# First FFN of a two-layer backbone on one core: modulation sums by accumulating DMAs, paced accumulations, and a joint K sweep

## The chip, the cores and the metric

The kernel runs on one core of one Trainium2 chip. The metric is the device time of one execution in microseconds (us). The kernel before took 1245.69 us, the median of three runs (1245.28 to 1246.67). The profile comes from a further execution of the same program; its own time stands in the table below.

## The reference, cut to what matters

Two streams of 256 tokens, `x` (latent) and `ctx` (context), go through layer 0, and `x` alone goes on through layer 1. Each layer has a half-step SwiGLU FFN, a token mixer and another half-step FFN, and everything is fp32. What this case is about is the conditioning: each layer has nine modulation vectors of 1024 elements for each stream, made from one long weight matrix.

```python
s_c, s_cc = jax.nn.silu(c), jax.nn.silu(c_ctx)          # 1024 elements each
m  = (s_c  @ ada_w[i] + ada_b[i]).reshape(B, N_MOD, 1, D)   # ada_w[i]: 1024 x 9216
mc = (s_cc @ ada_w[i] + ada_b[i]).reshape(N_MOD, D)         # for the context
x = half_step_ffn(x, m[:, 0], m[:, 1], m[:, 2], ...)        # shift, scale, gate
```

`half_step_ffn` modulates its input by shift and scale, computes `(silu(a) * u) @ w_out` from `h @ w_in = [a, u]` (2816 columns each), and adds the result, times gate, to the scaled residual before a layer norm.

## The kernel before, in words

**Splits.** Matmuls run on fp32r parts: each weight tile that a DMA loads is split into a high part by ScalarE (ACT) and a low part by VectorE (DVE), and three matmuls (high by high, low by high, high by low) make one product. Such a split of 128 x 512 costs one ACT and one DVE instruction. `wunit` (L185) loads a unit of 512 KB into a raw buffer (4 of them) and splits it into a pair of buffers `wh`, `wl` (5 pairs); in this stage every sixth unit goes to an extra pair `whx`, `wlx` instead, which `ext[0]` turns on (L202).

**The first FFN.** After a start in which the first two modulation vectors are computed by TensorE (PE), the 22 column blocks of `w_in` are worked in panels (`F0`, L714) of 3, 2, 2, 1 and then seven times 2 blocks, and these in three parts: 8, 8 and 6 blocks. For each block `j` there are two PSUM banks, z = 0 (the half for silu) and z = 1. A bank sums over 8 values of K, 3 matmuls each, so a block takes 48 matmuls. The loop (L784) sweeps all of K for z = 0 and then all of K for z = 1. `f0_gate` (L736) then makes silu on ACT, the product on DVE (L739), and the split of the result (L118 on ACT, L119 on DVE). After a part, `out_gemm` multiplies its blocks by rows of `w_out`: for each of two column halves n and four token tiles t, 4, 4 or 3 units of 6 matmuls, and then a residual on DVE (L419, and L422 or L424). Every 6 matmuls call `tick()`.

**The background.** Beside this, a generator (`stream`, L368) makes 14 more modulation vectors in 7 groups of two. `ada` (L287) loads `ada_w` in pieces of 128 x 1024 (512 KB, tile `ar`, 3 buffers), and DVE multiplies each by 128 elements of silu(c) and adds it to an accumulator of 128 x 1024 (`acc`, 2 buffers): two instructions of 128 x 512 for each vector and piece (L305 for the first piece, L307 for the others). Groups 0, 1 and 2 hold the same vector for the two streams, and so 8 pieces; groups 3 to 6 hold two different vectors of `x`, and so 16 pieces. Once both accumulators of a group are complete, PE sums over their 128 partitions by multiplying with a matrix of ones (L342; four matmuls in the code, which the profile shows as eight, on four column groups), DVE adds the bias (L343), and SP writes the rows to DRAM scratch `scr` (L345). The generator advances by a rate per tick: 0.45, then 0.44 from the end of the first part (L796), then 0.6 once three groups are made (`ADA_FAST`).

**What sets the order.** PE's order is the order of the code. The other engines are ordered by a list scheduler, which goes by priority (`high_priority`), by its own estimate of times, and by `issue_after`, which only fixes that an instruction is queued behind another on its engine. Every engine runs its queue in order, so one that waits holds all behind it. SP issues nearly every DMA: weights, `ar` pieces, and the reads of `scr`. Such a read is `fold_cols` (L387, `mrow<-scr`), which fetches shift and scale as rows, and the two gate loads (L793). GpSimd (POOL) is nearly idle in this stage; it has two small operations for each layer norm (L435, L436) from the third part on.

## Time and profile before

| | before |
|---|---|
| median of three runs (lowest to highest) | 1245.69 us (1245.28 to 1246.67) |
| time of the profiled execution | 1244.82 us |
| its span on the core | 1243.0 us |
| granted TensorE clock | 0.998 |
| PE busy | 1225.6 us (99%) |
| DVE busy | 963.7 us (78%) |
| ACT busy | 645.1 us (52%) |
| POOL busy | 84.4 us (7%) |
| DMA queue of SP | 274.54 MB, 73.0% of 16 engines |

The span runs from the first to the last instruction of the program; the time of the execution is 1.82 us longer. A busy PE is no proof of a PE at its peak, since matmuls are pipelined and their ends are modelled: the distance from the start of one matmul to the start of the next tells whether PE waited. In a row of the trace, `out<-in` names tiles, `x8` counts instructions, and a bracket at the end gives idle time before the row and what ended it. The landing of a DMA is counted from its issue.

### The profile page before, as it was taken

Reading aid. Unit: us, or ns where it says so; the run is one execution under the profiler, and the core shown is the slowest. Engines: PE = TensorE matmul, PEld = TensorE weight load, DVE = VectorE, ACT = ScalarE, POOL = GpSimd, SP = SyncE. Lnnn points to the kernel's source line nnn. Section 1 sums busy time; section 2 is a strip of 40 time slices with the busy share of each in tenths; the row PEclk is TensorE's granted clock in tenths of the full one; section 3 lists DMA queues with packets and bytes.
Section 4 is the critical chain, followed back from the end, with each engine's and each line's share of the span. In section 5 each row is a group of like instructions: output and inputs, shape, how many; then the busy total and the mean of one; then the engine's idle time right before and its main releaser. Section 6 shows DMA issues by size and latency. Waiting matters only on the chain.

```text
span 1243.0 us, 17234 instructions
## 1 busy us (share of the span) xinstructions
PE 1225.6 (99%) x5794; PEld 996.8 (80%) x5794; DVE 963.7 (78%) x1675; ACT 645.1 (52%) x1233; POOL 84.4 (7%) x93
## 2 busy tenths in 40 slices
PE   8999999999999999999999999999999999999997
PEld 6887778778778878777788888888888887888886
DVE  3699997888868876888877677877867798878646
ACT  2433132322325556587778635668645644677631
POOL 0000000000001011120000020020200120000200
PEclk9999999999999999999999999999999999999999
DMA  9886678878852654554899957889877765899741
GB/s 315 287 248 228 192 237 286 271 257 273 298 172 75 180 115 88 122 106 137 263 299 310 270 201 243 231 249 312 261 264 226 226 214 153 220 298 271 250 155 68
DMA packets 232304, 275.67 MB, mean 222 GB/s; under 512 B 59622, under 2 KB 178910, under 8 KB 232216
## 3 DMA queue, kind: packets, MB, share of 16 engines
q1 hardware_dynamic: 232020, 274.54, 73.0%
q8 instruction: 45, 0.74, 0.2%
q14 instruction: 43, 0.35, 0.1%
q0 software_dynamic: 160, 0.02, 0.1%
q10 hardware_dynamic: 36, 0.02, 0.0%
HBM read 265.27 MB, written 2.20 MB: 215 GB/s over the span
## 4 chain that ended last, share of the span: by engine, by line
PE 88%; DVE 5%; ACT 3%; DMA 2%; issue 1%; SPq 0%; POOL 0%; DVEq 0%; ACTq 0%
PE f L729 19%; PE w L170 17%; PE w L171 17%; PE w L173 17%; PE wc L170 2%; PE wc L173 2%; PE wc L171 2%; PE wkv L170 1%; PE wkv L171 1%; PE wkv L173 1%; PE hT L454 1%; PE ada L658 1%; ACT pr L1032 1%; PE S L1024 1%; DVE wkvl L219 1%
## 5 line engine op out<-in xcount | busy, mean ns | idle before, releaser
L219 DVE TENSOR_TENSOR w1l<-w1r,w1h 128x512 fp32r<-128x512 f32 (+1 forms) x352 | 231.2, 700 | 44.8 <-ACT w1h L216 43.9
L216 ACT ACTIVATE w1h<-w1r 128x512 fp32r<-128x512 f32 (+1 forms) x352 | 198.3, 618 | 115.2 <-PE w L173 52.4
L170 PE MATMUL w<-w1h,hTh 128*128 128x512 f32 x528 | 206.2, 391 | 1.2 <-ACT hTh L118 1.2
L171 PE MATMUL w<-w1l,hTh 128*128 128x512 f32 x528 | 205.6, 389 | 0.0
L307 DVE SCALAR_TENSOR_TENSOR acc<-ar,cst,acc 128x512 f32<-128x512 f32 x266 | 190.2, 759 | 12.5 <-DMA ar<-in_ada_w_dram 12.4
L170 PE MATMUL w<-w2h,gh 128*128 128x512 f32 (+1 forms) x446 | 173.4, 389 | 0.0
L171 PE MATMUL w<-w2l,gh 128*128 128x512 f32 (+1 forms) x446 | 172.3, 387 | 0.0
L216 ACT ACTIVATE w2h<-w2r 128x512 fp32r<-128x512 f32 x176 | 101.5, 624 | 135.2 <-PE w L173 99.6
L173 PE MATMUL w<-w1h,hTl 128*128 128x512 f32 x528 | 162.7, 389 | 0.0
L219 DVE TENSOR_TENSOR w2l<-w2r,w2h 128x512 fp32r<-128x512 f32 x176 | 113.6, 686 | 57.7 <-ACT w2h L216 56.6
L173 PE MATMUL w<-w2h,gl 128*128 128x512 f32 (+1 forms) x446 | 136.1, 386 | 0.0
L729 PE MATMUL f<-h0h,w1h 128*128 128x512 f32 x352 | 132.7, 393 | 1.2 <-ACT w1h L216 0.8
L729 PE MATMUL f<-h0l,w1h 128*128 128x512 f32 x352 | 133.1, 391 | 0.0
L729 PE MATMUL f<-h0h,w1l 128*128 128x512 f32 x352 | 132.8, 390 | 0.0
L170 PEld LDWEIGHTS w<-w1h,hTh 128*128 128x128 f32 x528 | 99.1, 188 | 22.4 <-ACT hTh L118 2.1
L173 PEld LDWEIGHTS w<-w1h,hTl 128*128 128x128 f32 x528 | 99.0, 188 | 21.0 <-DVE hTl L119 0.4
L171 PEld LDWEIGHTS w<-w1l,hTh 128*128 128x128 f32 x528 | 99.1, 188 | 20.6 <-DVE w1l L219 0.3
L170 PEld LDWEIGHTS w<-w2h,gh 128*128 128x128 f32 x446 | 83.8, 188 | 19.3 <-issue 1.7
L171 PEld LDWEIGHTS w<-w2l,gh 128*128 128x128 f32 x446 | 83.8, 188 | 17.1 <-DVE w2l L219 0.6
L173 PEld LDWEIGHTS w<-w2h,gl 128*128 128x128 f32 x446 | 83.3, 188 | 17.1
L729 PEld LDWEIGHTS f<-h0h,w1h 128*128 128x128 f32 x352 | 66.0, 189 | 18.9 <-issue 3.4
L729 PEld LDWEIGHTS f<-h0l,w1h 128*128 128x128 f32 x352 | 65.6, 188 | 14.2 <-issue 0.8
(197 smaller groups left out, 1766.0 us busy)
## 6 DMA issues: line engine op xcount, KB each, us to landing
w1r<-in_ffn_w_in_dram SPq DMA_DIRECT2D x340, 256.0 KB
ar<-in_ada_w_dram SPq DMA_DIRECT2D x128, 512.0 KB
w2r<-in_ffn_w_out_dram SPq DMA_DIRECT2D x88, 512.0 KB
ar<-in_ada_w_dram SPq DMA_DIRECT2D x32, 256.0 KB
wkvr<-in_na_w_qkv_dram SPq DMA_DIRECT2D x32, 256.0 KB
wcr<-in_sc_w_in_dram SPq DMA_DIRECT2D x32, 256.0 KB
wqr<-in_na_w_qkv_dram SPq DMA_DIRECT2D x8, 512.0 KB
wor<-in_na_w_out_dram SPq DMA_DIRECT2D x8, 512.0 KB
```

The source lines that it names most:

```text
L170: nc.tensor.matmul(ps, lh, rh, start=first and i == 0, stop=False)
L171: nc.tensor.matmul(ps, lh, rl, start=False, stop=False)
L173: nc.tensor.matmul(ps, ll, rh, start=False, stop=last and i == n - 1)
L216: last_split[:] = [nc.scalar.activation(hi[:, a:a + m // W_HI], raw[:, a:a + m // W_HI], AF.Copy)]
L219: last_lo[:] = [nc.vector.tensor_tensor(out=lo[:, a:b], in0=raw[:, a:b], in1=hi[:, a:b].bitcast(F32), op=ALU.subtract)]
L307: nc.vector.scalar_tensor_tensor(out=a, in0=src, scalar=sc, in1=a, op0=ALU.mult, op1=ALU.add)
L454: nc.tensor.transpose(ps[:, k * P:(k + 1) * P], z[h][:, k * P:(k + 1) * P], ident)
L658: nc.tensor.matmul(ps[o:o + 32, 0:m], cst[:, a * kt + i, :], w[:, i, j, :], start=(a == 0 and i < 2), stop=(a == last and i >= kt - 2))
L729: nc.tensor.matmul(ps, w, hT0[k][part == 1], start=(k == part == 0), stop=(k == KC - 1 and part == 1))
L1024: nc.tensor.matmul(banks[i], (qh, qh, ql)[f][ps, qs], (kh, kl, kh)[f][ps, :], start=f == 0, stop=f == 2)
L1032: nc.scalar.activation(pr, S, AF.Exp, bias=mx[:, 0:1], accum_out=mx[:, 1:2])
```

## The change

1. **Five sums become trees.** Groups 1 to 5 (`BY_TREE`) no longer use PE. Once an accumulator is complete, POOL issues a DMA that adds its partitions 64 to 127 onto 0 to 63, then 32 to 63 onto 0 to 31, and so on to one row: 7 levels, each waiting for the level before. An eighth DMA adds the row onto `scr`. For the two accumulators of groups 1 and 2 the levels alternate.
2. **Bias.** `scr` is filled with `ada_b` by three DMAs after the start stage (one of layer 1 moves there from later). Groups 0 and 6 keep the ones matmuls, but DVE only copies the result, and POOL writes it to `scr` by two accumulating DMAs. The tiles `adab` and `adar` go.
3. **Pace.** Accumulations in this stage are queued behind the latest gate product or residual in the order of the code (`pace`). An accumulation also comes one piece later than its load (`ADA_LAG` now holds from the start).
4. **Joint sweep.** A block now takes both banks and alternates z after every two values of K.
5. **Buffers.** `acc` and `ar` have 4 buffers instead of 2 and 3; the extra pair `whx`, `wlx` is off in this stage.
6. **Rates.** 0.64 instead of 0.6 after three groups, 0.4 instead of 0.44 after the first part; a group has three steps without a load (group 6 four) where it had four.

```diff
-ADA_SLOW, ADA_FAST, ADA_SLOWEST = 3, 0.6, 0.13
+ADA_SLOW, ADA_FAST, ADA_SLOWEST = 3, 0.64, 0.13
+BY_TREE = (1, 2, 3, 4, 5)
-    ext = [1, 0]
+    ext = [0, 0]
...
-                for i in gate_ins + (last_lo if on_pool[0] else []):
+                for i in gate_ins + (last_lo if on_pool[0] else pace):
                     st.enter_context(tc.issue_after(i.ins))
...
-                        acc[i] = hp.tile([P, D], F32, tag="acc", bufs=2, name=nm("acc"))
+                        acc[i] = hp.tile([P, D], F32, tag="acc", bufs=2 if on_pool[0] else 4, name=nm("acc"))
...
+            if k == KC - 1:
+                ready = [(vec, acc[i]) for i, vec in enumerate(vecs) if vec[:2] == (l, m)]
+                if on_pool[0]:
+                    sums.extend(ready)
+                elif made[0] in BY_TREE:
+                    n = P // 2
+                    while n:
+                        for _, a in ready:
+                            nc.gpsimd.dma_start(a[0:n], a[n:2 * n], accum_op=ALU.add)
+                        n //= 2
+                    for (l, m, v), a in ready:
+                        nc.gpsimd.dma_start(scr[l][v:v + 1, m * D:(m + 1) * D], a[0:1], accum_op=ALU.add)
...
-                w = hp.tile([P, D], F32, tag="ar", bufs=3, name=nm("ar"))
+                w = hp.tile([P, D], F32, tag="ar", bufs=3 if on_pool[0] else 4, name=nm("ar"))
...
-                if len(loaded) > (ADA_LAG if gate_ins else 0):
+                if len(loaded) > ADA_LAG:
...
+        for _ in range(3 if made[0] else 2):
+            yield 1
+        if made[0] in BY_TREE:
+            return
...
-        nc.vector.tensor_tensor(out=rows[:32 * n], in0=ps[:32 * n], in1=bt[:32 * n], op=ALU.add)
+        nc.vector.tensor_copy(rows, ps)
...
-            nc.vector.scalar_tensor_tensor(out=t, in0=ps, scalar=wgt, in1=gate, op0=ALU.mult, op1=ALU.mult)
+            pace[:] = [nc.vector.scalar_tensor_tensor(out=t, in0=ps, scalar=wgt, in1=gate, op0=ALU.mult, op1=ALU.mult)]
...
-        nc.vector.tensor_tensor(out=t, in0=t, in1=bk[1], op=ALU.mult)
+        pace[:] = [nc.vector.tensor_tensor(out=t, in0=t, in1=bk[1], op=ALU.mult)]
...
+    for l, v, r in ((0, 0, slice(2 * D, 9 * D)), (0, 1, slice(2 * D, 5 * D)), (1, 0, slice(0, 9 * D))):
+        sync.dma_start(scr[l][v, r].rearrange("(a b) -> a b", a=16), ada_b[l, r].rearrange("(a b) -> a b", a=16))
...
-                    bk = []
-                    for z in range(2):
-                        bk.append(mmb("f0", z))
-                        for k in range(0, KC, 2):
+                    bk = [mmb("f0", z) for z in range(2)]
+                    for k in range(0, KC, 2):
+                        for z in range(2):
                             f0_mm(bk[z], p, units, j, z, (k, k + 1))
                             tick()
...
-            background[1] = 0.44
+            background[1] = 0.4
```

Three pieces of the engines' queues follow, as the two programs have them; numbers in names tell buffers apart.

PE, at the sum of group 0, before. `f` are the banks of the first product, `h0h` and `h0l` the split input, `w1h` and `w1l` the split weights:

```order
L729 MATMUL f_160_955<-h0l_432,w1h_871 128x512
L729 MATMUL f_160_955<-h0h_453,w1h_871 128x512
L729 MATMUL f_160_955<-h0h_453,w1l_872 128x512
L729 MATMUL f_160_955<-h0l_454,w1h_871 128x512
L342 MATMUL ada_975<-acc_715,ones 32x512 x2
L342 MATMUL ada_975<-acc_718,ones 32x512 x2
L729 MATMUL f_160_955<-h0h_549,w1h_880 128x512
L729 MATMUL f_160_955<-h0h_549,w1l_881 128x512
```

PE, at the same sum, after:

```order
L733 MATMUL f_159_954<-h0l_181,w1h_852 128x512
L733 MATMUL f_159_954<-h0h_251,w1h_852 128x512
L733 MATMUL f_159_954<-h0h_251,w1l_853 128x512
L733 MATMUL f_159_954<-h0l_252,w1h_852 128x512
L346 MATMUL ada_963<-acc_733,ones 32x512 x2
L346 MATMUL ada_963<-acc_736,ones 32x512 x2
L733 MATMUL f_160_955<-h0h_180,w1h_852 128x512
L733 MATMUL f_160_955<-h0h_180,w1l_853 128x512
```

The sum comes 12 matmuls earlier than before (after 294 of the `f` matmuls, not 306). Of the six sums that follow it before, only that of group 6 is left after.

POOL, from the end of the start stage to the second tree, before (`srow` is a constant, `rs` belongs to the first layer norm):

```order
L281 MEMSET mrow_87 128x128
L330 MEMSET adab_926 128x512
L1173 MEMSET srow 128x128
L435 TENSOR_TENSOR rs_3347<-mv_3345,lnc 128x1
L436 TENSOR_TENSOR rs_3347<-rs_3347,lnc 128x1
```

The same place after, with the last rows of the tree of group 1 and the first of group 2:

```order
L317 DMA acc_1002<-acc_1002 2x1024
L317 DMA acc_999<-acc_999 1x16x64
L317 DMA acc_1002<-acc_1002 1x16x64
L320 DMA scr_118<-acc_999 16x1x64
L320 DMA scr_118<-acc_1002 16x1x64
L317 DMA acc_1313<-acc_1313 64x1024
L317 DMA acc_1316<-acc_1316 64x1024
L317 DMA acc_1313<-acc_1313 32x1024
L317 DMA acc_1316<-acc_1316 32x1024
```

Where POOL's queue had nothing, it now has 84 DMAs ahead of the first layer norm: 80 of the trees and 4 of groups 0 and 6.

SP, at the first read of a sum by `fold_cols` (`mrow<-scr`), before:

```order
L316 DMA ar_1432<-in_ada_w_dram 128x1024
L393 DMA mrow_86<-scr_118 8x128
L393 DMA mrow_87<-scr_118 8x128
L316 DMA ar_1453<-in_ada_w_dram 128x1024
L316 DMA ar_1472<-in_ada_w_dram 128x1024
L211 DMA w1r_1673<-in_ffn_w_in_dram 128x2x256
```

The same read after:

```order
L326 DMA ar_1459<-in_ada_w_dram 128x1024
L326 DMA ar_1484<-in_ada_w_dram 128x1024
L212 DMA w1r_1688<-in_ffn_w_in_dram 128x2x256 x2
L397 DMA mrow_86<-scr_118 8x128
L397 DMA mrow_87<-scr_118 8x128
L326 DMA ar_1620<-in_ada_w_dram 128x1024
L212 DMA w1r_1697<-in_ffn_w_in_dram 128x2x256 x2
L212 DMA w1r_1706<-in_ffn_w_in_dram 128x2x256 x2
```

The read waited for a write by SP itself and now waits for the tree of group 1; most weights of the second panel of the next part (`w1r_1697`, `w1r_1706`) are queued behind it.

More of the change, by code (lines that the diff above doesn't have):

```diff
@@ L281, in backbone_kernel @@
         nc.gpsimd.memset(z, 0.0)
-    bias_rows = []
     on_pool = [False]
     sums, last_gate = [], []
-    gate_ins = []
+    gate_ins, pace = [], []
     def ada(vecs):
@@ L308, in accumulate @@
                                                            op0=ALU.mult, op1=ALU.add)
-            if on_pool[0] and k == KC - 1:
-                sums.extend((vec, acc[i]) for i, vec in enumerate(vecs) if vec[:2] == (l, m))
+            if k == KC - 1:
[10 more added lines that the diff above has]
+                        nc.gpsimd.dma_start(scr[l][v:v + 1, m * D:(m + 1) * D], a[0:1], accum_op=ALU.add)
         loaded = []
@@ L326, in ada @@
             return
-        n = 2 * len(vecs)
-        if not bias_rows:
-            bias_rows.append(hp.tile([P, 512], F32, tag="adab", name=nm("adab")))
-            nc.gpsimd.memset(bias_rows[0], 0.0)
-        bt = bias_rows[0]
-        for i, (l, m, v) in enumerate(vecs):
-            sync.dma_start(bt[64 * i:64 * i + 64:32], ada_b[l, m * D:(m + 1) * D].rearrange("(a b) -> a b", b=512))
-        yield 1
-        yield 1
-        yield 1
-        rows = hp.tile([P, 512], F32, tag="adar", name=nm("adar"))
+        for _ in range(3 if made[0] else 2):
+            yield 1
+        if made[0] in BY_TREE:
+            return
+        rows = sp.tile([P, 512], F32, tag="s2", bufs=S2, name=nm("adar"))
         ps = tpb("ada")
@@ L342, in ada @@
                 nc.tensor.matmul(ps[32 * j:32 * j + 32, :], ones, acc[i][:, h * 512:(h + 1) * 512], start=True, stop=True)
-        nc.vector.tensor_tensor(out=rows[:32 * n], in0=ps[:32 * n], in1=bt[:32 * n], op=ALU.add)
+        nc.vector.tensor_copy(rows, ps)
         for i, (l, m, v) in enumerate(vecs):
-            sync.dma_start(scr[l][v, m * D:(m + 1) * D].rearrange("(a b) -> a b", b=512),
-                           rows[64 * i:64 * i + 64:32, :])
+            nc.gpsimd.dma_start(scr[l][v, m * D:(m + 1) * D].rearrange("(a b) -> a b", b=512),
+                                rows[64 * i:64 * i + 64:32, :], accum_op=ALU.add)
         yield 1
@@ L597, in backbone_kernel @@
     w_in, w_out = ffn_w_in[0, 0], ffn_w_out[0, 0]
-    ab0 = hp.tile([P, D], F32, tag="acc", bufs=2, name="ab0")
+    ab0 = hp.tile([P, D], F32, tag="acc", bufs=2 if on_pool[0] else 4, name="ab0")
     nc.vector.memset(ab0, 0.0)
@@ L616, in start_tile @@
             return hp.tile([P, 2, 512], F32, tag="pt", bufs=4, name=nm("ar")).rearrange("p a b -> p (a b)")
-        return hp.tile([P, D], F32, tag="ar", bufs=3, name=nm("ar"))
+        return hp.tile([P, D], F32, tag="ar", bufs=4, name=nm("ar"))
     marks = []
@@ L1161, in backbone_kernel @@
     on_pool[0] = True
-    sync.dma_start(scr[1][0, 4 * D:9 * D].rearrange("(a b) -> a b", a=16), ada_b[1, 4 * D:9 * D].rearrange("(a b) -> a b", a=16))
     ext[0] = 2
```

## The prediction

> **What bounds the kernel now.** I read the page first, then the stretches of the first FFN, then PE's rows one by one.
>
> ```profile
> span 1243.0 us, 17234 instructions
> PE 1225.6 (99%) x5794; PEld 996.8 (80%) x5794; DVE 963.7 (78%) x1675; ACT 645.1 (52%) x1233; POOL 84.4 (7%) x93
> ```
>
> PE lacks only 17.4 us of the whole span. The view of stretches cuts out four parts of the first FFN, each between two sums on PE; its columns are PE, weight loads, DVE, ACT and POOL busy, then clock, DMA share and GB/s.
>
> ```profile
> 59.00:95.50 36.50, 36.50 (x163) 30.23 (x162) 33.38 (x53) 12.90 (x22) 0.00 (x0) 1.00 0.79 246
> 222.00:266.00 44.00, 44.00 (x196) 36.41 (x195) 37.47 (x60) 12.26 (x21) 0.00 (x0) 1.00 0.86 287
> 268.00:312.00 44.00, 44.00 (x195) 36.41 (x195) 37.91 (x61) 10.32 (x19) 0.00 (x0) 1.00 0.82 264
> 314.00:359.90 45.90, 45.90 (x203) 37.99 (x204) 37.09 (x60) 14.78 (x27) 0.00 (x0) 1.00 0.76 250
> ```
>
> PE is busy throughout, DVE for 81 to 91%, and POOL not at all. Busy alone could hide waits, so here are PE's own rows around the sum of group 0, and the row of all the sums:
>
> ```profile
> 94.67 0.39 PE L729 MATMUL f<-h0h,w1l 128*128 128x512 f32 x1
> 94.90 0.39 PE L729 MATMUL f<-h0l,w1h 128*128 128x512 f32 x1
> 95.13 0.39 PE L729 MATMUL f<-h0h,w1h 128*128 128x512 f32 x1
> 95.36 0.39 PE L729 MATMUL f<-h0h,w1l 128*128 128x512 f32 x1
> 95.58 0.39 PE L729 MATMUL f<-h0l,w1h 128*128 128x512 f32 x1
> 95.90 1.06 PE L342 MATMUL ada<-acc,ones 128*32 128x512 f32 x8
> 96.90 0.50 PE L729 MATMUL f<-h0h,w1h 128*128 128x512 f32 x1
> 97.23 0.39 PE L729 MATMUL f<-h0h,w1l 128*128 128x512 f32 x1
> ...
> L342 PE MATMUL ada<-acc,ones x56: 592/605/617, 95.9 to 360.8; 128*32 128x512 f32 x56
> ```
>
> From 94.67 to 95.58 are four steps, so matmuls start 0.228 us apart, though each shows 0.39 us. The stage is bound by PE's issue rate and nothing else: whatever is taken from PE here shortens the kernel, and whatever is taken from another engine does not, as long as it keeps up.
>
> **The change part by part.**
>
> *Five sums leave PE.* From 95.58 to 97.23 are 1.65 us, in which two matmuls would start without the sum (0.46 us). One sum costs 1.19 us, more than its row's 1.06, because the matmuls on both sides of it are stretched. The row counts 56 matmuls, eight for each of seven groups, so the five others are alike: 5 x 1.19 = **6.0 us less on PE**. These lie on the path entirely.
>
> *The sum of group 0 comes earlier.* It stands 12 matmuls earlier on PE, so PE is there at 95.9 - 12 x 0.228 = 93.2 us. Its last twelve accumulations now stand between two gate products on DVE, those that the trace of before has at 83.34 and 92.00:
>
> ```profile
> 83.34 0.68 DVE L739 TENSOR_TENSOR sil<-sil,f 128x512 f32<-128x512 f32 x1
> ...
> 92.00 0.69 DVE L739 TENSOR_TENSOR sil<-sil,f 128x512 f32<-128x512 f32 x1 [1.00 <-PE f L729]
> ...
> 124.88 1.40 DVE L307 SCALAR_TENSOR_TENSOR acc<-ar,cst,acc 128x512 f32<-128x512 f32 x2
> 126.20 0.68 DVE L419 SCALAR_TENSOR_TENSOR res<-w,gate 128x512 f32<-128x512 f32 x1
> 126.81 0.68 DVE L219 TENSOR_TENSOR w2l<-w2r,w2h 128x512 fp32r<-128x512 f32 x1
> 127.41 0.68 DVE L424 SCALAR_TENSOR_TENSOR x<-x,res 128x512 f32<-128x512 f32 x1
> ...
> 149.26 0.68 DVE L419 SCALAR_TENSOR_TENSOR res<-w,gate 128x512 f32<-128x512 f32 x1
> ...
> 170.61 0.69 DVE L739 TENSOR_TENSOR sil<-sil,f 128x512 f32<-128x512 f32 x1 [0.26 <-PE f L729]
> ...
> 207.44 0.68 DVE L739 TENSOR_TENSOR sil<-sil,f 128x512 f32<-128x512 f32 x1
> ```
>
> An accumulation takes 0.70 us of DVE's time (1.40 for two), another operation 0.60 (126.20 to 126.81 to 127.41). So they end at 83.34 + 0.6 (product) + 0.6 (split of the result) + 12 x 0.70 = 92.9 us, just before PE comes. The cost lies between 0 and 1.5 us; I take **0.5**.
>
> *Joint sweep.* PE never waits for a bank or a unit, so it wins nothing by itself. It covers the loss of the extra buffer pair: with K swept once for both banks, unit u of a panel is released in the second block at 10.9 + 2.73u us (12 matmuls a unit, 48 a block) and its successor in the ring of five is wanted about 10.9 us later, where two sweeps took a unit each 1.37 us. Its price is that silu starts when both banks are done, 0.60 us later in the chain silu, product, high, low (about 2.5 us in all). Within a part nothing is behind that; at a part's end the last block is first needed after 14 matmuls (third part, 3.2 us) or 20 (4.6 us). DVE's queue may be late by a few instructions there: 0 to 1 us; I take **0.2**.
>
> *Pace.* An accumulation now waits on DVE for the latest product or residual, and behind it are queued weight splits and further accumulations. Between two products PE takes 48 x 0.228 = 10.9 us. DVE has in that time, at 0.64 pieces a tick and 8 ticks, at most 5.1 pieces x 2 x 0.70 = 7.2 us, two units' low parts (4 x 0.60 = 2.4) and 1.2 for the product and the split: 10.8 us at most, and 9.6 with the three steps in nineteen that load nothing. It just keeps up. In the first part, where a piece feeds two streams, both kernels ask for more (0.45 x 8 x 4 x 0.70 = 10.1 of accumulations alone while a group loads), and the trace of before has DVE at 33.38 of 36.50 us there and no wait of PE. So 0 is taken, and the rest is a rival below. That five bias additions go (0.6 us each) and 0.4 replaces 0.44 only moves DVE's slack.
>
> *Trees.* They run on POOL, idle here, and nobody on PE waits for them. The nearest row is the accumulating DMA of later layers, one row of 4 KB (L357):
>
> ```profile
> L357 POOL DMA_DIRECT2D scr<-red x5: 997/997/1118, 727.6 to 1156.2; - x5
> ...
> DMA to landing us min/median/max: 2.3/2.8/5.0
> ```
>
> POOL is held 1.0 us for an issue, and landing takes 2.8 us. A tree is eight such steps in series, each for two accumulators in groups 1 and 2: 8 x 2.8 = 22 us, between 8 x 2.3 = 18 and 8 x 5.0 = 40; the first levels carry 256 and 128 KB each and not 4, which I allow 5 us for, from the 2 us that a piece of 512 KB takes at 246 to 287 GB/s. I take 28 us a tree. Who waits for it: (a) SP's first `mrow<-scr` row. Group 1's last accumulation now stands ahead of the residual at 126.20; SP comes to that row once the accumulations behind the residual at 149.26 have freed a load buffer, 23 us later, and then stands still for some 5 us. The weights behind it are for the panel that starts after the gate product following 170.61, at about 182 us: over 50 us after the tree began. (b) DVE: with four buffers the first accumulation of group 3, queued behind 170.61, needs group 1's, 44 us after that tree began. (c) Group 4's first accumulation, behind 207.44, needs group 2's, whose tree follows group 1's on POOL: two trees in 81 us. All hold at 28 us; the cost is **0**.
>
> A page speaks against this. The Trainium skill, "SBUF — State Buffer", section "Who interferes with whom", says that descriptor generation on GpSimd is starved while a DVE copy or `tensor_scalar` runs in a two-port mode. The L357 row, issued among DVE work, does not show it (997 to 1118 ns). By the rule each of 16 DMAs of a tree could wait for one such operation, which would lengthen the tree, not PE's path, and leave the sum as it is.
>
> *Bias, and behind the stage.* Three small DMAs on SP replace fourteen. The copy of two sums instead of an addition is off the path. In the attention that follows, the scheduler's order changes a little:
>
> ```profile
> 424.01 1.45 DVE L830 TENSOR_TENSOR x<-x,lng 128x512 f32<-128x512 f32 x2 [5.55 <-DMA lng<-in_ln_g_dram]
> ...
> 436.71 0.50 PE L1024 MATMUL S<-kTl,qTh 64*128 64x512 f32 x2 [0.84 <-DVE kTl L119]
> ```
>
> DVE stands 5.55 us for a load, and later PE waits 0.84 us for DVE. After the change three small operations stand ahead of that wait instead of behind it, which could remove the 0.84 or, if the load comes later, double it: -0.84 to +0.84; I take **-0.4**.
>
> *Sum.* -6.0 + 0.5 + 0.2 - 0.4 = -5.7 us. The profiled execution took 1244.82 us (span 1243.0 and 1.8 us around it), 0.9 below the median. The changed one should have a span of 1237.3; against the median of 1245.69 that is **1240.0 us**. With the bounds of the terms (-6.84 to -2.66) and the scatter of the three runs, this case reaches from 1238.4 to 1243.2.
>
> **The rivals.** About 0.2%, 2.5 us, is what a measurement of this kernel can tell from no change.
>
> *A: DVE takes PE's place as the bound (gain eaten).* For: 10.8 of 10.9 us is no slack, and if an accumulation took its full 0.74 us the interval would be 11.2; demand on DMA rises as well, to 0.64 x 512 KB per 1.37 us, or 246 GB/s, and 96 for weights (two units in 10.9 us): 342 GB/s, near the most that a stretch shows:
>
> ```profile
> 650.00:660.00 10.00, 10.00 (x46) 8.28 (x45) 8.15 (x15) 8.10 (x15) 0.00 (x0) 1.00 1.12 347
> ```
>
> Against: loadless steps give back 1.2 us per interval on average, and weights go ahead by priority. It needs lags beyond the 10.9 us that the ring allows, at two or three places; 1 to 2 us each leaves 1243 to 1248 us.
>
> *B: the trees are too slow (slower than before).* At L us per level, two trees take 16L, and (c) holds to 81 us, plus some 10 us that the weights behind it can be late: it decides from L = 5.1 to 5.7 us. At L = 6, group 4's first accumulation waits 96 - 81 = 15 us, of which 4 reach PE; groups 5 and 6 wait alike, as single trees then follow faster than POOL clears them. Some 12 us less the 6 gained gives 1252 us, and L = 7 some 25 us more than that. For: 64 rows are added, not one, beside DMA engines 76 to 86% busy. Against: the slowest of five landings is 5.0.
>
> *C: more is gained than PE's sums.* The change would have to free a wait that PE's spacing of 0.228 us doesn't show, in the start or the attention: 1236.5 to 1238.4.
>
> *D: the change doesn't do what it says.* If PE still ran the sums, the time would stay at 1245.7; PE's order has two sums left and not seven, so this gets 1 in 100.
>
> **How the numbers follow.** Forecast 0.62, A 0.18, B 0.14, C 0.05, D 0.01. The likeliest is 1240.0 us. The range from 1238.4 to 1246.0 holds the forecast and most of A. Faster by over 0.2% (below 1243.2) are the forecast, C and a little of A: 0.70. Within 0.2% are the rest of A and D: 0.16. Slower is B: 0.14.
>
> **What the profile will show.** Right: two `ada` sums on PE with `acc` instead of seven, matmuls 0.228 us apart between 60 and 380 us, and the layer norms behind the stage about 5 to 6 us earlier. A tree's DMAs land 2.8 to 4 us apart, and a tree ends within 44 us. Wrong by A: gaps of PE in this stage that end on `w1l`, `w2l` or `acc`. Wrong by B: DVE idle ahead of the first accumulation of a group, ended by a DMA of POOL, or SP standing at `mrow<-scr` until weights are late. Wrong in group 0's term: a gap ahead of the first sum of more than 1.5 us.

## The result, and the profile after

| | before | after |
|---|---|---|
| median (lowest to highest, runs) | 1245.81 us (1245.28 to 1246.67, 4) | 1254.80 us (1251.68 to 1256.74, 4) |
| ratio, with its 95% interval | | 1.0072 (1.006 to 1.0084) |
| span of the profiled execution | 1243.0 us | 1252.4 us |

The change costs 9 us, and the forecast of 1240.0 us, with a range up to 1246.0, was wrong in its sign. The head of the page of the changed kernel:

```profile
span 1252.4 us, 17274 instructions
PE 1225.1 (98%) x5754; PEld 997.2 (80%) x5754; DVE 960.1 (77%) x1670; ACT 645.1 (52%) x1233; POOL 148.9 (12%) x176
```

PE has 40 matmuls fewer, the five sums, but 27.3 us of the span without work where it had 17.4. The view of PE's waits from 200 to 445 us (what waited, for what; us in all, times, longest) says where:

```profile
PE w L171 <- ACT gh L119: 2.5, 1, 2.5
PE S L1029 <- DVE kTl L120: 1.9, 1, 1.9
PE wq L172 <- DVE wql L220: 1.3, 1, 1.3
PE ada L346 <- DVE acc L307: 0.2, 1, 0.2
PE w L174 <- DVE gl L120: 0.2, 1, 0.2
```

The first stands at the end of the second part, the second and third in the attention behind the stage. Before, only the second was there, with 0.84 us. The stretches, cut like those shown of before:

```profile
58.00:94.50 36.50, 36.50 (x163) 30.23 (x162) 32.74 (x54) 12.34 (x22) 0.00 (x0) 1.00 0.78 255
216.00:251.00 35.00, 35.00 (x156) 29.00 (x155) 31.94 (x52) 12.37 (x22) 8.81 (x11) 1.00 0.96 319
268.00:312.00 44.00, 44.00 (x196) 36.44 (x195) 40.00 (x66) 12.59 (x22) 9.55 (x12) 1.00 0.96 305
```

PE is still full inside these stretches, and POOL, idle before, is busy for 22 to 25% of the second and third. The DMA engines went from 82 to 86% busy to 96%.

The surest reading comes from comparing the two traces matmul by matmul: the k-th matmul on a bank is the same work in each, so the difference of its start times shows what has been won or lost by then. Each column is such a kernel's profiled execution against before's, in us; the last four columns are experiments that follow (1, 17, 13 and 16), where their names are explained.

```
time before, at                  after  no trees  0.57 only  turn+drain  turn+drain+pair+0.57
  96.9  behind group 0's sum     +1.86     +0.33      +0.47       +0.11      +0.68
 253.3  end of part 2            -1.96     +0.19      -3.34       -2.93      -3.14
 254.4  5 matmuls on             +1.29     +0.19      -3.34       +0.80      -3.14
 314.6  behind the sum of group 5 -1.11    +0.21      -5.78       -0.20      -5.57
 361.9  behind that of group 6   +0.82     +0.22      -5.77       -0.19      -5.57
 402.5  first matmuls of wq      +2.61     +2.01      -3.95       +1.59      -5.57
 440.4  behind the first S       +5.23     +2.75      -2.72       +2.97      -6.35
1234.9  last matmul              +6.12     +4.13      -1.62       +3.27      -6.23
end of the span                  +9.4      +4.0       +1.6        +3.2       -6.3
```

From 96.9 to 361.9 five sums should give 6.0 us; after gives 1.04. About 5 us are lost there again, 3.3 at 254 and 1.9 at the sum of group 6. Another 5.3 us go behind the stage, where the change edits nothing that PE runs, and 3.3 between the last matmul and the end.

**The end of the span.** The lines of the program's end, first before, then after (line, kind, count: ns shortest/median/longest, first and last start):

```profile
L1290 POOLq DRAIN  x3: 40/102/1408, 1237.2 to 1242.8; - x3
```

```profile
L1294 POOLq DRAIN  x3: 46/102/8273, 1243.3 to 1252.1; - x3
```

POOL's last wait for its own work takes 8.27 us instead of 1.41. It ends 3.3 us after SP has seen the stores land, and the span ends with it.

**The end of the second part.** ACT and DVE of the changed kernel from 245 us:

```profile
245.83 0.60 ACT L742 ACTIVATE sil<-f 128x512 f32<-128x512 f32 x1
247.24 1.15 ACT L217 ACTIVATE w2h<-w2r 128x512 fp32r<-128x512 f32 x2 [0.81 <-PE f L733]
253.52 0.63 ACT L119 ACTIVATE gh<-sil 128x512 fp32r<-128x512 f32 x1 [5.12 <-DVE sil L743]
```

```profile
248.95 1.41 DVE L307 SCALAR_TENSOR_TENSOR acc<-ar,cst,acc 128x512 f32<-128x512 f32 x2
250.27 1.29 DVE L220 TENSOR_TENSOR w2l<-w2r,w2h 128x512 fp32r<-128x512 f32 x2
251.48 1.41 DVE L307 SCALAR_TENSOR_TENSOR acc<-ar,cst,acc 128x512 f32<-128x512 f32 x2
252.80 0.68 DVE L743 TENSOR_TENSOR sil<-sil,f 128x512 f32<-128x512 f32 x1
253.40 1.29 DVE L220 TENSOR_TENSOR w2l<-w2r,w2h 128x512 fp32r<-128x512 f32 x2
```

Silu is ready at 246.4, but its product starts at 252.80: DVE works without a pause through accumulations and weight splits queued ahead of it. That delay from silu to product is the best gauge of DVE. For the eight blocks of the second part it is 0.9, 0.8, 3.1, 3.7, 5.1, 5.6, 5.8 and 6.4 us: it opens and doesn't close again in this part. DVE's own rows show what opens it, and the landing of the tree levels belongs to it:

```profile
189.35 1.41 DVE L307 SCALAR_TENSOR_TENSOR acc<-ar,cst,acc 128x512 f32<-128x512 f32 x2 [1.88 <-DMA ar<-in_ada_w_dram]
193.12 0.88 DVE L305 TENSOR_SCALAR acc<-ar,cst 128x512 f32<-128x512 f32 x2 [2.36 <-DMA ar<-in_ada_w_dram]
...
216.88 0.88 DVE L305 TENSOR_SCALAR acc<-ar,cst 128x512 f32<-128x512 f32 x2 [6.38 <-DMA scr<-acc]
```

```profile
DMA to landing us min/median/max: 2.0/4.8/8.4
```

DVE stands twice for a late load, and then 6.38 us for an accumulator whose tree isn't done: it is the first of group 4, which takes the buffer that the tree of group 2 has to give back. My first theory was that POOL's queue is the cause: the trees of groups 1 and 2 run as two pairs, but those of groups 3 to 5 as six single ones, so that eight chains of eight steps follow each other nearly end to end, from 127 to 374 us, and from 213 us on one ends only every 26 us, with a new accumulator complete every 22. It is tested below, and falls in part.

### The profile page after: what moved, and what is told of

Its sections match the earlier page's. It is cut to its first block, busy times and chain, and to the rows that moved or that the text cites. A ratio compares the mean times of both kernels' runs of the same rounds, so it can differ in the third digit from the quotient of the medians.

```text
span 1252.4 us, 17274 instructions
## 1 busy us (share of the span) xinstructions
PE 1225.1 (98%) x5754; PEld 997.2 (80%) x5754; DVE 960.1 (77%) x1670; ACT 645.1 (52%) x1233; POOL 148.9 (12%) x176
## 4 chain that ended last, share of the span: by engine, by line
PE 69%; DMA 14%; DVE 9%; ACT 3%; issue 3%; POOL 1%; SPq 0%; DVEq 0%; ACTq 0%; POOLq 0%
PE w L171 15%; PE w L172 15%; PE w L174 15%; DMA acc<-acc 11%; PE f L733 9%; PE wkv L171 2%; PE wkv L172 2%; PE wkv L174 2%; DVE acc L307 1%; DMA wcr<-in_sc_w_in_dram 1%; PE wc L171 1%; PE wc L174 1%; PE wc L172 1%; DMA ar<-in_ada_w_dram 1%; DVE w1l L220 1%
## 5 line engine op out<-in xcount | busy, mean ns | idle before, releaser
L307 DVE SCALAR_TENSOR_TENSOR acc<-ar,cst,acc 128x512 f32<-128x512 f32 x266 | 185.9, 746 | 5.6 <-DMA ar<-in_ada_w_dram 5.3
L220 DVE TENSOR_TENSOR w2l<-w2r,w2h 128x512 fp32r<-128x512 f32 x176 | 118.0, 712 | 57.6 <-ACT w2h L217 56.5
L317 POOL DMA_DIRECT2D acc<-acc x70 | 56.2, 827 | 195.2 <-DMA acc<-acc 156.6
```

Of the source, the lines that this page charges most:

```text
L220: last_lo[:] = [nc.vector.tensor_tensor(out=lo[:, a:b], in0=raw[:, a:b], in1=hi[:, a:b].bitcast(F32), op=ALU.subtract)]
L307: nc.vector.scalar_tensor_tensor(out=a, in0=src, scalar=sc, in1=a, op0=ALU.mult, op1=ALU.add)
L317: nc.gpsimd.dma_start(a[0:n], a[n:2 * n], accum_op=ALU.add)
```

## The experiments

Kernel 1 is the kernel of experiment 1, and so on. Before, run beside them on the same chips, had medians from 1244.96 to 1245.63 us. Ratios are to it.

**1. No trees.** `BY_TREE = ()`.

> No group is summed by a tree; all seven sums are on PE again, everything else of the change stays (bias added by DMA, pace, joint sweep, four accumulators and load buffers, rates 0.64 and 0.4). Theory T (eight chains of tree levels run one behind another on POOL from 169 to 374 us, so accumulators and the modulation rows come late; and POOL's last drain, 7.4 us behind its last operation instead of 0.5, is the end of the span): the waits of PE at 254, 404 and 440 us go, the drain is short again, five sums come back at 1.2 us: 1245 to 1247.5 us. Rival P (pace and joint sweep alone put DVE behind): PE still waits about 2.5 us for gh at the end of the second part and the layers behind stay late; only the tail (3.3 us) goes and 6 us come back: 1250 to 1258 us.

Measured: 1248.79 us, ratio 1.0028 (1.0017 to 1.004), between the two. In the stage nothing is lost (column "no trees": +0.22 at 361.9), so pace, joint sweep, bias and rate 0.64 cost nothing there without trees: the delay from silu to product is 0.8 to 1.1 us throughout the second part. But the waits in the attention stay, which neither theory had right (PE's waits from 60 to 445 us):

```profile
PE S L1029 <- DVE kTl L120: 1.6, 1, 1.6
PE wq L172 <- DVE wql L220: 1.4, 1, 1.4
```

So 3 to 4 us of the loss have nothing to do with trees: 3.2 by the medians, 4.1 at the last matmul of the table.

**2. Trees for groups 1 and 2 alone.** `BY_TREE = (1, 2)`.

> Trees for groups 1 and 2 alone, the sums of groups 3 to 5 on PE. Theory T: the second tree ends near 215 us with nothing behind it, PE's waits at 254, 404 and 440 us go; two sums less on PE (2.4 us); POOL's last drain behind some 50 software DMAs instead of 89 takes about 4 us, no longer than the stores' landing: 1243 to 1245.5 us. Rival P (pace and joint sweep): waits as in the changed kernel, 1252 to 1258 us.

Measured: 1250.36 us, ratio 1.0036 (1.0024 to 1.0049). That is above the theory's range and below the rival's. The wait at 254 is gone, and those in the attention are there (1.3 and 2.1 us). But the stage isn't free of loss. The delay from silu to product opens as in the changed kernel (3.1 us at 193), and PE pays for it at the sum of group 3 (211 to 215 us): against before it falls back there by 2.9 us, after which DVE is on time again (1.2 us at 228). Ahead of that, SP stands for 10.0 us at a read of `scr` that waits for the second tree (it is issued at 205.7), the DMA engines are 4% busy from 200 to 204 us, and DVE, its queue worked off, has to wait for a load:

```profile
209.82 1.41 DVE L307 SCALAR_TENSOR_TENSOR acc<-ar,cst,acc 128x512 f32<-128x512 f32 x2 [4.45 <-DMA ar<-in_ada_w_dram]
```

So here a late load comes from SP standing for a tree, and not from full DMA engines. The last drain is as forecast, 3.9 us behind POOL's last operation with 47 software DMAs, and hidden.

**3. A reduce on POOL instead of a tree.**

```diff
...
+                        red = hp.tile([P, D], F32, tag="red", name=nm("red"))
+                        nc.gpsimd.partition_all_reduce(red, a, P, ReduceOp.add)
+                        nc.gpsimd.dma_start(scr[l][v:v + 1, m * D:(m + 1) * D], red[0:1], accum_op=ALU.add)
...
```

> Groups 1 to 5 are summed on POOL by a partition reduce (6.1 to 9.5 us each in later layers) and one accumulating DMA, in place of a tree; three accumulators instead of four make room for its result. Theory T: ten reduces take 61 to 95 us of POOL between 125 and 330 us, so nothing queues, DVE doesn't wait for an accumulator, 19 software DMAs leave the drain short: 1239 to 1242 us, below the kernel before. Rival P: DVE is late by itself, 1248 to 1252 us. Rival S (POOL and DVE hinder each other): reduces of over 20 us or accumulations of over 0.8 us on DVE, and as late as the trees: 1248 to 1255 us.

Measured: 1264.56 us, ratio 1.0158 (1.0145 to 1.0172). Rival S, but in another way than it says, and dearer than its range. The reduces are as short as elsewhere. Each holds up one DVE instruction that runs beside it: POOL and DVE in the same 10 us (an accumulation's first step takes 0.48 us otherwise):

```profile
171.66 8.41 POOL L316 PARTITION_ALL_REDUCE red<-acc  x1 [27.68 <-DVE acc L307]
```

```profile
174.01 0.67 DVE L740 TENSOR_TENSOR sil<-sil,f 128x512 f32<-128x512 f32 x1
174.61 5.73 DVE L305 TENSOR_SCALAR acc<-ar,cst 128x512 f32<-128x512 f32 x2
```

Ten reduces made ten DVE instructions 3.6 to 5.0 us long, a `tensor_scalar`, a `scalar_tensor_tensor` or a `tensor_tensor`. The kernel before had this too: the five reduces of its later layers go with five DVE instructions of 3.1 to 4.6 us. The Trainium skill, "SBUF — State Buffer", section "Who interferes with whom", calls the port pair that DVE shares with GpSimd an exclusive lock. This trace agrees in kind, but the hold is shorter than the reduce beside it, which takes 6.1 to 8.6 us. The other half of that section, which the prediction weighed, is not seen: POOL's 70 issues of tree DMAs took 0.79 us in the median and 1.15 at most.

**4. Before, with 84 software DMAs.** One row of 512 bytes each, issued by POOL at the start.

```diff
+    junk = tc.dram_tile([8, P], F32, name="junk")
+    for i in range(84):
+        nc.gpsimd.dma_start(junk[i % 8:i % 8 + 1], mrow[0][0:1], accum_op=ALU.add)
```

> The kernel before with 84 accumulating DMAs of one row of 512 bytes each, issued by POOL at the start of the kernel to a buffer that nothing reads. Theory T (the drain's length goes with the number of software DMAs): POOL's last drain ends about 7 us behind its last operation, 3.3 us behind the stores' landing, PE as before: 1249 us. Rival (the drain waits for bytes, or for something that the trees leave late): 1245 to 1246.5 us, drain 0.5 us behind the last operation.

Measured: 1248.78 us, ratio 1.0027 (1.0017 to 1.0038). Theory T: the tail is the number of software DMAs, whatever they carry and however long ago they landed. The drains at its end:

```profile
L1293 POOLq DRAIN  x3: 40/102/8268, 1237.0 to 1245.8; - x3
```

With 5, 19, 47 and 89 of them the drain ends 0.50, 1.65, 3.93 and 7.36 us behind POOL's last operation: 0.082 us for each. The landing of the stores hides 3.9 us of it, about 47 DMAs.

**5. No trees, and the extra pair of weight buffers back.** `ext = [1, 0]`, and three buffers each for `acc` and `ar`.

> No trees (all seven sums on PE), and the extra pair of weight buffers is back in the first FFN, its room taken from one accumulator and one load buffer (three of each). Pace, bias by DMA, joint sweep and rates stay as in the changed kernel. Theory X (what is left of the loss without trees is the missing pair: the fourth piece of the first attention weights is asked for at 378 us instead of 364, behind the modulation rows): it is asked for at about 364 us again, PE's wait for wql (1.4 us) goes, its wait for kTl falls from 1.6 to 0.8 us: 1245 to 1246.5 us. Rival Y (pace, bias or the sweep shifts the order in the attention): waits as without the pair, 1248 to 1249.5 us.

**6. Before, without the extra pair.** `ext = [0, 0]`, nothing else.

> The kernel before with one edit: no extra pair of weight buffers in the first FFN. Theory X: the fourth piece of the first attention weights comes some 14 us later, PE waits about 1.4 us for wql and 1.6 to 2.1 for kTl, nothing or little in the FFN itself: 1247.5 to 1250 us. Rival Y: no such waits, 1245 to 1246.5 us.

Measured: 5 has 1245.87 us, ratio 1.0003 (0.9994 to 1.0011); 6 has 1250.23 us, ratio 1.0041 (1.0027 to 1.0056). PE's waits in kernel 6 from 240 to 445 us:

```profile
PE wq L171 <- DVE wql L219: 1.3, 1, 1.3
PE w L170 <- ACT gh L118: 0.9, 1, 0.9
PE S L1024 <- DVE kTl L119: 0.9, 1, 0.9
```

Theory X holds from both sides for the late piece and for `wql`. For `kTl` it holds in 5, where the wait is 0.9 us, but not in 6, where it is 0.9 too, hardly more than before, and not the 1.6 to 2.1 that was expected: that the time of 6 came out near its range is in part luck. Of the 3.7 us by which its last matmul is late, 1.5 stand ahead of the attention, 1.1 of them from 253 us, where PE waits for `gh`, and 2.2 behind the stage. SP's queue of kernel 1 and of kernel 5 shows the mechanism:

```profile
358.42 5.81 SPq L212 DMA_DIRECT2D wqr<-in_na_w_qkv_dram  x3
370.20 0.69 SPq L397 DMA_DIRECT2D mrow<-scr  x2
...
377.71 0.39 SPq L212 DMA_DIRECT2D wqr<-in_na_w_qkv_dram  x1
```

```profile
356.29 8.26 SPq L212 DMA_DIRECT2D wqr<-in_na_w_qkv_dram  x4
370.53 0.65 SPq L397 DMA_DIRECT2D mrow<-scr  x2
```

Without the pair there is room for three pieces of the attention's first weights ahead of the modulation rows, not four. The fourth comes 14 us later, and all that stands behind it on SP is later too, the layer norm's rows `lng` by 3.5 us (issued at 421.3 us against 417.8). DVE has both late in its queue, and PE waits for `wql` and, in kernel 1, longer for `kTl`.

**7. An early drain, not held in place.** `nc.gpsimd.drain()` behind the first attention.

> The changed kernel with one more drain on POOL, emitted behind the first attention, long after the trees. Theory T1 (a drain waits 0.08 us for each software DMA issued since the drain before it): the early one takes 5 to 7 us on an idle POOL, the last one ends under 1.5 us behind POOL's last operation, and the span ends with the stores' landing: 1251 to 1252 us. Rival T2 (each drain goes through all software DMAs of the program again, or something else makes it long): the last drain ends 7.4 us behind the last operation as before, 1254 to 1256 us.

Measured: 1254.27 us, ratio 1.0072 (1.006 to 1.0084). Not a test: the scheduler put the drain at 1.01 us, ahead of all DMAs. It serves as a second profile of the changed kernel, and repeats the waits for `gh` (2.6 us), `wql` and `kTl`.

**8. The pair back, trees for groups 3 and 4 alone.** As 5, with `BY_TREE = (3, 4)`.

> The extra pair is back, three accumulators, three load buffers, and trees for groups 3 and 4 alone (four single trees, about 25 us each, accumulations about 21 us apart; 47 software DMAs). Theory (pair, queue of trees and tail are the whole loss): two sums less on PE (2.4 us), a queue of at most 16 us on POOL, which the third accumulator covers, tail hidden: 1242.5 to 1244 us, below the kernel before. Rival (a tree holds an accumulator that DVE wants, or SP's modulation rows): PE waits in the second part, 1245 to 1248 us.

Measured: 1263.97 us, ratio 1.0151 (1.0134 to 1.0168). The rival. DVE waits 16 us for trees and 17 us for loads, and PE stands 4.6 us for `gh` and 7.1 at a sum. The first of the four trees took 43 us, not 25.

**9. Drains held in place.**

```diff
-                nc.gpsimd.tensor_tensor(out=warm, in0=red[0:1, 0:1], in1=lnc[0:1, 0:1], op=ALU.add)
+                last = nc.gpsimd.tensor_tensor(out=warm, in0=red[0:1, 0:1], in1=lnc[0:1, 0:1], op=ALU.add)
+                with queued([last]):
+                    nc.gpsimd.drain()
```

> The changed kernel with a drain on POOL behind each of its five later sums (from about 740 to 1170 us), queued there, so that it can't be moved ahead of the trees. Theory T1 (a drain waits 0.08 us for each software DMA issued since the drain before it): the first of them takes 5 to 7 us, the others under 1 us, the last one of the span ends under 1.5 us behind POOL's last operation: 1251 to 1252 us. Rival T2 (each drain goes through all software DMAs again): each of the five takes 7 us and the last one too: 1254 to 1256 us.

Measured: 1249.94 us, ratio 1.0041 (1.0028 to 1.0054). Theory T1, and 1 us below its range (group 6's sum costs 0.9 us more than its matmuls here, not 1.9). The drains behind the sums, and those of the program's end:

```profile
L365 POOLq DRAIN  x5: 8240/8567/15884, 731.9 to 1159.7; - x5
```

```profile
L1296 POOLq DRAIN  x3: 40/102/989, 1241.5 to 1247.0; - x3
```

The first ends 7.0 us behind the operation ahead of it and the four others 0.15 us, the rest of their length being that operation. The last ends 0.1 us behind it. A drain pays for each software DMA once, wherever it stands.

**10. Trees of a group in turn.** The two trees of groups 3 to 5 alternate level by level too: five chains instead of eight.

```diff
+                    held.extend(ready)
+                    ready = held
+                    if len(ready) < len(vecs):
+                        return
...
-                        for _, a in ready:
-                            nc.gpsimd.dma_start(a[0:n], a[n:2 * n], accum_op=ALU.add)
+                        for _, a in reversed(ready):
+                            with queued(level):
+                                level = [nc.gpsimd.dma_start(a[0:n], a[n:2 * n], accum_op=ALU.add)]
```

> The changed kernel with the two trees of a group level by level in turn for groups 3 to 5 too, so that POOL runs five chains of levels instead of eight; the first accumulator of a group then waits about 21 us for the second. Theory Q (the length of POOL's queue is what DVE and SP wait for): chains of 32 to 46 us end at about 345 us instead of 374, SP no longer stands at the modulation rows, DVE's waits for accumulators shrink, PE's wait of 2.5 us at the end of the second part goes: 1250.5 to 1253 us. Rival H (each tree holds its accumulators, and now for longer): DVE waits longer ahead of groups 5 and 6, PE as long or longer: 1254 to 1260 us.

Measured: 1249.48 us, ratio 1.0042 (1.0028 to 1.0055), better than theory Q's range, and its means are half right. The last chain's last step is issued at 336 us, SP no longer waits at the rows behind the stage, the wait at the sum of group 6 is gone. The wait for `gh` is still 1.6 us, and in kernel 13, which has the same trees, 2.7.

**11. The pair back, trees for group 5 alone.** As 5, with `BY_TREE = (5,)`.

> No trees but those of group 5, the extra pair back, three accumulators and three load buffers. Theory (a tree is free where nobody waits for its accumulator, its rows or POOL): one sum less on PE (1.2 us): 1244 to 1245.2 us. Rival (with three accumulators the trees of group 5 hold group 6 up, as trees of groups 3 and 4 held what followed them): DVE idle ahead of group 6's accumulations, 1246 to 1252 us.

Measured: 1246.67 us, ratio 1.0008 (1.0 to 1.0017). No wait of PE in the stage, and no gain either. The median lies in the rival's range, but the rival's sign is missing: no accumulation of DVE waits for a tree. A sum's 1.2 us is at the edge of what this can tell, so it decides nothing.

**12. In turn, drains, and the pair, for one load buffer less** (and `S2 = 6`, `tmp` 2).

> All three repairs at once: levels of a group's two trees in turn (five chains), drains on POOL behind its later sums, and the extra pair of weight buffers, its 8 KB taken from one load buffer, one of seven temporaries (s2) and one of three (tmp). Theory (queue of trees, lost pair and drain are the whole loss, and they add): from the interleaved kernel's 1249.5 us the tail (3.2 us) and the pair (3 to 4 us) go: 1241 to 1244.5 us, below the kernel before. Rival (the room that is taken is missed: DVE or the loads wait as they did with three load buffers and trees of groups 3 and 4): waits of PE at 250 to 310 us, 1245 to 1256 us.

Measured: 1256.15 us, ratio 1.0097 (1.0079 to 1.0114). The rival. DVE's longest waits in it, from 60 to 400 us (us in all, times, longest):

```profile
DVE acc L307 <- DMA ar<-in_ada_w_dram: 32.9, 23, 5.7
```

Without trees three load buffers were enough at 0.64 (kernel 5). That they are too few beside trees isn't the whole cause, as kernel 14 shows.

**13 and 14. In turn and drains; then the pair besides, for temporaries** (`ext = [1, 0]`, `S2 = 4`, `tmp` 2).

> The changed kernel with the trees of a group in turn (five chains) and drains on POOL behind its later sums; no extra pair, four accumulators and four load buffers as in the changed kernel. Theory (queue, tail and pair add up): the interleaved kernel's 1249.5 us less the tail of 3.2 us: 1245.5 to 1247 us, the kernel before's time, with five sums less on PE eaten by what the pair's loss costs. Rival (they do not add): 1248 to 1251 us.

> As that one, with the extra pair besides, and its 8 KB taken from temporaries only (s2 from seven to four, tmp from three to two), so that four accumulators and four load buffers stay. Theory (in the kernel with all three repairs the missing load buffer was what DVE waited for): no waits on loads of over 10 us in all, PE's waits for w2l and w2h at 250 to 260 us go, the fourth piece of the first attention weights is asked for at about 360 us: 1242 to 1245 us. Rival (temporaries are missed: silu, its product or the attention's rows wait for a buffer): new waits of PE spread over the stages, 1247 to 1260 us.

Measured: 1248.94 us, ratio 1.0034 (1.0021 to 1.0047), and 1248.67 us, ratio 1.0025 (1.0016 to 1.0035). Both missed, and lie in the ranges of their rivals: PE's wait for `gh` at the end of the second part is 2.7 us in 13 and 4.9 in 14, though POOL's queue is short. The queue is not the whole cause. In 14 DVE still waits 23 us for loads, with four load buffers; the fourth piece is asked for at 367 us and PE's wait for `wql` is gone.

**15 and 16. The same two kernels, at 0.57 instead of 0.64.**

> The kernel with the trees in turn and the early drains, and one edit: after three groups the background advances by 0.57 a tick instead of 0.64. Theory L (what is left at the end of the second part, PE waiting 2.7 us for gh, comes from accumulations and loads at 0.64 besides the trees: DMA 97 to 100% busy from 200 to 256 us, DVE 95% busy, so that a wait is never made up): at 11% less demand PE's wait there falls below 1 us: 1245.5 to 1247.5 us. Rival M (it comes from accumulators held by trees, whatever the rate): the wait stays over 2 us, 1248 to 1251 us.

> As that one with the extra pair of weight buffers, its room from temporaries (s2 four, tmp two). Theory L and the pair together: PE's 7 us of waits at 249 to 258 us fall below 2 us, no wait at wql: 1242 to 1245 us. Rival (temporaries are missed, or trees hold accumulators): waits at the end of the second part of over 4 us, 1247 to 1250 us.

Measured: 15 has 1244.85 us, ratio 0.9997 (0.9988 to 1.0006); 16 has **1238.74 us, ratio 0.9949 (0.9935 to 0.9962)**, 6 us below before and more than the theory hoped for. Theory L. Head of the page of 16, its stretches from 200 us, and its tree levels:

```profile
span 1236.7 us, 17279 instructions
PE 1220.2 (99%) x5754; PEld 996.7 (81%) x5754; DVE 959.3 (78%) x1670; ACT 645.2 (52%) x1233; POOL 152.0 (12%) x176
```

```profile
200.00:216.00 16.00, 16.00 (x72) 13.24 (x71) 11.06 (x19) 4.59 (x8) 6.37 (x8) 1.00 1.00 346
216.00:240.00 24.00, 24.00 (x108) 19.88 (x107) 20.39 (x34) 8.13 (x14) 6.56 (x8) 1.00 0.95 292
240.00:256.00 16.00, 16.00 (x72) 13.26 (x71) 14.86 (x24) 4.59 (x8) 5.00 (x7) 1.00 0.99 344
```

```profile
DMA to landing us min/median/max: 1.9/5.2/8.8
```

PE has no wait between 60 and 445 us that the profile lists, not even the 0.84 us of before. The levels land no faster than in the changed kernel and the DMA engines are as full: full engines and 5 us a level alone don't stop PE.

**17. The rate alone.** The changed kernel with 0.57.

> The changed kernel with one edit: 0.57 a tick instead of 0.64 after three groups. Eight chains on POOL, the lost pair and the long last drain stay. Theory L (the rate decides): PE's wait for gh at the end of the second part (2.5 us) falls below 1 us as it did with the trees in turn, the rest stays: 1250.5 to 1252.5 us. Rival Q (POOL's eight chains decide): SP still stands at the modulation rows for over 8 us and PE's wait stays over 2 us: 1253 to 1256 us.

Measured: 1248.37 us, ratio 1.002 (1.0011 to 1.0029). Theory L, by more than it said: from 96.9 to 361.9 five sums give 6.24 us (column "0.57 only"). Q's sign is there, SP stands up to 19.8 us at the rows, but in the stage it reaches neither DVE nor PE: DVE waits once for a tree, 1.6 us, and the delay from silu to product is 0.8 to 1.6 us in the second part. ACT at the same place as above:

```profile
244.45 0.60 ACT L742 ACTIVATE sil<-f 128x512 f32<-128x512 f32 x1 [0.16 <-PE f L733]
245.86 1.16 ACT L217 ACTIVATE w2h<-w2r 128x512 fp32r<-128x512 f32 x2 [0.81 <-PE f L733]
246.92 0.62 ACT L119 ACTIVATE gh<-sil 128x512 fp32r<-128x512 f32 x1
```

So a long queue on POOL alone doesn't make the loss in the stage: it is there at 0.57 without the loss, and the loss is there in 13 with a short one. At 0.64 without trees (kernel 1) DVE is on time throughout the second part; at 0.57 with the same trees (kernel 17) it is too; with both it isn't. How a tree does it is less clear. In kernel 15, at 0.57 with the trees in turn, the delay still reaches 6.0 us at 235 and PE loses 1.7 us at 254.

## Why the prediction was wrong

- **Five sums leave PE, 6.0 us: right.** Kernels 16 and 17 gain 6.25 and 6.24 us in the stage by the table. In the changed kernel the same sums leave and 5 us come back.
- **Group 0's sum, 0.5 us: it cost nothing.** Each kernel of the table stands as far from before at 110 us, behind this sum, as at 90, ahead of it; the 0.14 us more in the row of 96.9 is only the place of before's own sum. The changed kernel's 1.72 us at both were there by 31 us, 1.44 of them from a late first load, which no other run shows.
- **Pace, 0 us: this step failed in the stage, together with the trees.** It counted 10.8 of 10.9 us and said that DVE "just keeps up". That is no slack, so a wait is carried on to the end of a part: the two late loads and the 6.38 us for a tree became 3.3 us of PE's time at 254 (`gh` and `gl`, with a slow start) and, with those that followed, 1.9 at the sum of group 6. Rival A named this mechanism, and priced it at 1243 to 1248 us; what it lacked is that the long waits come only with the trees (in kernel 1 DVE waits 1.2 us for a load at most). The 0.64 on the list of rates was the lever, and I priced it only by DVE's share.
- **Trees, 0 us: the bound was for the wrong trees.** 28 us a tree was fair for the first (31) and low for the second (42), as a level landed 4.8 us after issue and not 2.8. The test of who waits covered groups 1 and 2, and its (c) failed: group 4's first accumulation is ready at 210.5 us, 84 us after the first tree began, near the 81 forecast, but the buffer that it needs, group 2's, comes free only after 90, and DVE stands for 6.38 us. The six single trees of groups 3 to 5 were only looked at in rival B, for L = 6; at 4.8 they fall behind too, one ending every 26 us where an accumulator is complete every 22. Rival B's signs are all there. SP standing at the rows cost nothing in the stage in kernel 17, and 2.9 us in kernel 2.
- **Joint sweep "covers the loss of the extra buffer pair": this step failed behind the stage.** In the stage it holds (kernel 1: +0.22 us, where kernel 6, with two sweeps, loses 1.1). But the pair also held a piece of the attention's weights. Behind the stage kernel 6, which lacks nothing but the pair, loses 2.2 us, kernel 1 loses 3.9, kernel 5 with the pair nothing, and the changed kernel 5.3, 1.6 of them by a slow clock, below. I followed the buffers to the end of the stage that the edit is in, and not to the next load that takes them.
- **The attention's order, -0.4 with bounds of 0.84 either way: mis-sized.** I read the shifted order as a matter of three small operations. With the pair back the wait is 0.9 us (kernel 5), with the pair alone taken away it is 0.9 too (kernel 6), and with both the lost pair and the rest of the change it is 1.6 to 2.0 (kernels 1 and 17, and the changed one). What of the rest does this stays open.
- **Not in the sum at all: the end.** 84 more software DMAs lengthen POOL's last drain by 6.9 us, 3.3 of them beyond the stores' landing.

The sum as measured in the profiled execution, from the table: 1.86 at the start, 1.04 less in the stage (6.24 gained and 5.2 lost), 5.30 behind it, 3.3 at the end, together 9.4 us. The five sums alone come to 6.1 us between 110 and 380 us in kernels 16 and 17. Kernel 16 takes the three losses back and comes out at 1238.74 us, near the 1240.0 forecast for a change that had none.

What stays open: whether the two late loads that open DVE's delay in the changed kernel come from full DMA engines or from SP standing for other buffers, which no run took apart (in kernel 2 a later one came from SP); and why PE still waits 0.8 us for `gh` in 15 and not in 16, which has fewer temporaries and one pair more.

## What to carry to other kernels

An engine that just keeps up has no way to make up a wait: price a change that adds waits by the slack per interval, not by the busy share, and try a lower rate before a shorter wait. Follow a buffer that is taken away to whoever loads into it next, past the end of the stage. Count what a new kind of instruction leaves to the end of the program.

## What the runs showed of the hardware

- A drain on POOL took 0.082 us for each software DMA issued since the drain before it, even for DMAs that had landed a millisecond earlier (5, 19, 47, 89 DMAs: 0.50, 1.65, 3.93, 7.36 us).
- Behind a wait, PE's clock fell for a few us. The stretches from 436 us of the changed kernel, and PE's rows there:

```profile
436.00:440.00 4.00, 2.50 (x15) 1.66 (x13) 4.00 (x8) 2.56 (x4) 0.00 (x0) 1.00 0.68 210
440.00:444.00 4.00, 3.62 (x11) 2.52 (x12) 2.87 (x6) 1.24 (x3) 0.00 (x0) 0.60 0.99 311
```

```profile
440.38 0.50 PE L1029 MATMUL S<-kTl,qTh 64*128 64x512 f32 x2 [1.88 <-DVE kTl L120]
...
441.80 0.63 PE L172 MATMUL wkv<-wkvl,hTh 128*128 128x512 f32 x1
442.22 0.63 PE L171 MATMUL wkv<-wkvh,hTh 128*128 128x512 f32 x1
442.65 0.63 PE L172 MATMUL wkv<-wkvl,hTh 128*128 128x512 f32 x1
```

Matmuls start 0.427 us apart instead of 0.228, at a granted clock of 0.60 in that stretch: the wait of 1.88 us cost another 1.6 us (the table: from +3.67 at the first matmul behind it to +5.23). The Trainium skill, "TensorE: Matmul & The Clock Gate", section "Wait — 56ns, not 53.3ns?", gives 426.7 ns as the spacing of matmuls of 512 columns at half clock, and the trace agrees. Its section "HAM oscillation — how this bites in real kernels" puts the danger at pauses of over 3.4 us; here 1.88 us were enough, while 2.52 us at 254 in the same execution had no such tail. At the same place the clock fell behind 1.66 us in kernel 9 and not behind 2.02 and 2.56 us in kernels 17 and 15, so the length of the wait alone doesn't decide.
- A partition reduce on POOL of 6.1 to 8.6 us went with one DVE instruction beside it that took 3.6 to 5.0 us, ten times out of ten.
